# Last block's side work ordered behind four engines' queues, an earlier norm, another bank for the pooled map, and a tail reduction on TensorE

## The chip, the cores and the metric

The kernel runs on one core of a Trainium2 chip. TensorE (PE) multiplies, VectorE (DVE), ScalarE (ACT) and GpSimd (POOL) do the elementwise work, SyncE (SP) issues nearly all transfers. The metric is the device time of one execution in microseconds, as the median of several runs.

## What is computed

One decoder layer on 2048 tokens of width 1024, in float32:

```python
h = rmsnorm(x, norm1)
q, k, v, b_gate, c_gate, hc, p = split(h @ w_in)
attn = sliding_window_attention(q, k, v, sinks, rel_bias)   # window 128, 8 query heads, 2 kv heads
conv = b_gate * causal_conv3(c_gate * hc)
pool = (trailing_mean(p, windows 2/4/8/16) - p) @ pool_w * pool_scale
x = x + concat(attn, conv, pool) @ w_out
x = x + square(relu(rmsnorm(x, norm2) @ w1)) @ w2
out = rmsnorm(x, final_norm)
```

## The kernel before, in words

Every float32 matrix product is made of three TensorE products: an operand is split in a rounded part "hi" and a rest "lo", and `mm3` adds hi·hi, hi·lo and lo·hi in PSUM. ACT makes hi, POOL or DVE the rest. Everything is stored transposed: 128 channels on the partitions, tokens along the free axis.

The first stage goes over four blocks of 512 tokens (`b` = 0 to 3). In a block, `proj` makes 14 tiles in the order of IN_ORDER (k, q0, q1, then, counted by `n` = 0 to 10: v, q2, q3, p0, p1, C0, hc0, B0, C1, hc1, B1), of 24 products each. Attention goes along in eight units: after tile `n`, `att_scores` makes scores on PE and the softmax on DVE and ACT (L581, L588, exp on ACT at L590, L593, L594); two tiles later `att_trans` transposes the unit's probabilities into a `ps_tr` bank and splits them (L604, L607, L608), `att_av` multiplies by v (L615), and `att_out` writes the rows of `mxh` and `mxl` (L623 to L629). `do_pmix` multiplies the pooled values by `pool_w` into a `ps_tr` bank and writes two more rows of `mxh`, `mxl` (L707, L708). Then `out_proj` makes eight tiles, `c` = 0 to 7, each from all eight rows of `mxh` and `mxl`, adds x (L724) and stores to the DRAM tensors `x1s`. PSUM has three banks `ps_mm` for tiles of `proj` and `out_proj`, two `ps_tr`, one `ps_av`, and the score banks.

Between the `out_proj` tiles of block `b` stands the norm of block `b`+1: squares summed by DVE (L374), `norm_rstd` (PE sums over partitions into `pst`, L314; twelve small DVE operations), `row_store` and `norm_bcast` (through DRAM), and `norm_apply` for each of eight channel groups (DVE L404, ACT L405, DVE L406).

Block 3 has no next block. It carries other work for the MLP that follows: `first_rows` and `first_blocks(k, step)`, for `k` = 0 to 3. Step 0 loads four tiles `xb` from `x1s` of blocks 0 and 1, step 1 scales them (four DVE operations, L809), step 2 makes four differences (DVE, L763 with `xb`); the results are stored to `x2s`. FIRST gives for each `k` the tile `n` after which each step is traced. Within `out_proj` of block 3, `first_take` loads them again and splits them (L763 with `hhT`, `hhB`). LAST_DVE puts eight weight splits (L253) of block 3 on DVE instead of POOL.

The order on each engine is not that of the program. The framework schedules at build time with a timing model of its own: when an engine is free in the model, it takes the earliest traced instruction that is ready there, and the queues then run in that fixed order. `tc.issue_after(ins)` adds an edge from each instruction traced within it to `ins`, for instructions on the engine of `ins` alone. Before the change `ins` is the last product of `proj`, a PE instruction, while `first_rows` and `first_blocks` trace only on SP and DVE.

Then comes the MLP in a form with seven products (OPS); `norm2_take` loads its last two operands (T4, B22) once the first stage's memory is free (L965 to L967), and `norm2_rstd` sums block 3's squares (`acc` L732 of POOL). Last comes the second product; its last quarter (256 tokens) is followed by the final norm: four additions to `y` on DVE, four squares on ACT (L1136) and four additions on POOL into `acc3`, `final_rstd`, `final_bcast`, eight `final_mul` on DVE (L1152), each with its store on SP (L1156).

## Time and profile before

| | |
|---|---|
| median of 3 runs | 1938.14 us (1935.13 to 1943.75) |
| profiled execution | 1936.93 us, span 1935.2 us |
| busy: PE, DVE, ACT, POOL | 98%, 58%, 46%, 53% of the span |
| chain that ended last, by engine | PE 83%, DVE 7%, DMA 6%, issue 2% |
| blocks 1, 2 and 3, first product to first product of what follows | 175.88 to 327.52, 479.08 and 648.33 us |

A busy PE includes the pipelined ends of its products, so its share is not its efficiency. An idle time of an engine stands in brackets in a timeline row, with what ended it. The column PEclk of a stretch is the granted TensorE clock: 1.00 is 2.4 GHz, 0.50 is 1.2 GHz.

### The profile page before, as it was taken

Reading aid. Unit: us, or ns where it says so; the run is one execution under the profiler, and the core shown is the slowest. Engines: PE = TensorE matmul, PEld = TensorE weight load, DVE = VectorE, ACT = ScalarE, POOL = GpSimd, SP = SyncE. Lnnn points to the kernel's source line nnn. Section 1 sums busy time; section 2 is a strip of 40 time slices with the busy share of each in tenths; the row PEclk is TensorE's granted clock in tenths of the full one; section 3 lists DMA queues with packets and bytes.
Section 4 is the critical chain, followed back from the end, with each engine's and each line's share of the span. In section 5 each row is a group of like instructions: output and inputs, shape, how many; then the busy total and the mean of one; then the engine's idle time right before and its main releaser. Section 6 shows DMA issues by size and latency. Waiting matters only on the chain.

```text
span 1935.2 us, 25620 instructions
## 1 busy us (share of the span) xinstructions
PE 1892.6 (98%) x8507; PEld 1527.8 (79%) x8507; DVE 1123.6 (58%) x1423; ACT 895.9 (46%) x1640; POOL 1020.0 (53%) x748
## 2 busy tenths in 40 slices
PE   8999999999899999999999999999999999999997
PEld 5877887887687788888888888888888888888887
DVE  5785686585888577756574444442425264533465
ACT  5664674564367344554575545442323222225332
POOL 5666557565463655654464444434565665526521
PEclk9999999999899999999999999999999999999998
DMA  7327316425935779756685655578777566645344
GB/s 255 102 65 225 108 61 217 126 66 174 300 117 178 233 272 335 255 197 212 216 288 194 196 185 189 186 270 279 235 231 240 191 218 200 221 123 169 96 158 134
DMA packets 194136, 373.34 MB, mean 193 GB/s; under 512 B 22167, under 2 KB 30420, under 8 KB 194004
## 3 DMA queue, kind: packets, MB, share of 16 engines
q1 hardware_dynamic: 193768, 371.62, 59.6%
q8 instruction: 67, 1.10, 0.2%
q14 instruction: 65, 0.53, 0.1%
q10 hardware_dynamic: 236, 0.09, 0.0%
HBM read 248.41 MB, written 116.93 MB: 189 GB/s over the span
## 4 chain that ended last, share of the span: by engine, by line
PE 83%; DVE 7%; DMA 6%; issue 2%; ACT 1%; POOL 1%; SPq 1%; DVEq 0%; POOLq 0%; ACTq 0%
PE o L274 11%; PE o L275 11%; PE o L276 11%; PE bT L275 6%; PE bT L276 6%; PE bT L274 6%; PE bB L275 5%; PE bB L274 5%; PE bB L276 5%; PE pj L275 4%; PE pj L276 4%; PE pj L274 4%; DMA x1s<-xo 1%; PE pt L604 1%; DVE xl L406 1%
## 5 line engine op out<-in xcount | busy, mean ns | idle before, releaser
L253 POOL TENSOR_TENSOR wl<-wr,wh 128x512 fp32r<-128x512 f32 x354 | 499.2, 1417 | 502.4 <-ACT wh L252 462.1
L252 ACT CAST wh<-wr 128x512 fp32r<-128x512 f32 x416 | 254.3, 617 | 362.5 <-PE bT L275 66.9
L763 DVE TENSOR_TENSOR bl<-br,bh 128x1024 fp32r<-128x1024 f32 (+2 forms) x144 | 186.8, 1300 | 324.7 <-ACT bh L1111 323.8
L275 PE MATMUL o<-bl,wh 128*128 128x512 f32 (+1 forms) x960 | 363.4, 381 | 0.0
L276 PE MATMUL o<-bh,wl 128*128 128x512 f32 (+1 forms) x960 | 362.7, 381 | 0.0
L274 PE MATMUL o<-bh,wh 128*128 128x512 f32 (+1 forms) x960 | 351.1, 381 | 0.0
L275 PEld LDWEIGHTS o<-bl,wh 128*128 128x128 f32 x960 | 180.9, 188 | 38.3 <-DVE bl L763 0.2
L276 PEld LDWEIGHTS o<-bh,wl 128*128 128x128 f32 x960 | 180.8, 188 | 38.2
L274 PEld LDWEIGHTS o<-bh,wh 128*128 128x128 f32 x960 | 176.3, 188 | 38.0
L276 PE MATMUL bT<-hhT,wl 128*128 128x512 f32 x512 | 203.7, 398 | 0.0
L275 PE MATMUL bT<-hlT,wh 128*128 128x512 f32 x512 | 203.6, 398 | 0.0
L274 PE MATMUL bT<-hhT,wh 128*128 128x512 f32 x512 | 203.4, 398 | 0.0
L274 PE MATMUL pj<-xh,wh 128*128 128x512 f32 x440 | 176.7, 403 | 10.6 <-ACT wh L252 6.7
L275 PE MATMUL pj<-xl,wh 128*128 128x512 f32 x440 | 177.5, 403 | 6.1 <-DVE xl L406 5.8
L276 PE MATMUL pj<-xh,wl 128*128 128x512 f32 x440 | 176.2, 401 | 0.0
L253 POOL TENSOR_TENSOR wl<-s,wh 128x512 fp32r<-128x512 f32 x64 | 91.2, 1426 | 141.5 <-ACT wh L252 130.9
L252 ACT CAST wh<-s 128x512 fp32r<-128x512 f32 x64 | 39.7, 621 | 250.1 <-PE o L275 249.9
L275 PE MATMUL bB<-hlB,wh 128*128 128x512 f32 x384 | 152.3, 397 | 0.7 <-DVE hlB L967 0.7
L274 PE MATMUL bB<-hhB,wh 128*128 128x512 f32 x384 | 152.5, 397 | 0.0
L1111 ACT CAST bh<-br 128x1024 fp32r<-128x1024 f32 (+2 forms) x144 | 123.2, 857 | 63.3 <-PE o L276 57.6
L276 PE MATMUL bB<-hhB,wl 128*128 128x512 f32 x384 | 152.0, 396 | 0.0
L220 POOL TENSOR_TENSOR s<-wr,wr 128x512 f32<-128x512 f32 x64 | 128.5, 2008 | 14.9 <-DMA wr<-in_w_dram 10.2
(188 smaller groups left out, 3388.0 us busy)
## 6 DMA issues: line engine op xcount, KB each, us to landing
wr<-in_w_dram SPq DMA_DIRECT2D x256, 256.0 KB, 3.8
hop_T<-s SPq DMA_DIRECT2D x128, 256.0 KB, 3.1
wr<-in_win_dram SPq DMA_DIRECT2D x112, 256.0 KB, 4.4
hop_B<-h SPq DMA_DIRECT2D x96, 256.0 KB, 3.3
br<-hop_B SPq DMA_DIRECT2D x48, 512.0 KB, 4.4
br<-hop_T SPq DMA_DIRECT2D x48, 512.0 KB, 4.3
wr<-in_wout_dram SPq DMA_DIRECT2D x64, 256.0 KB, 2.9
wr<-ss_T SPq DMA_DIRECT2D x48, 256.0 KB, 2.8
```

Of the source, the lines that this page charges most:

```text
L220: gp.tensor_tensor(out=t, in0=a, in1=b, op=op)
L252: act.copy(hi, src)
L253: eng.tensor_tensor(out=lo, in0=src, in1=f32(hi), op=ALU.subtract)
L274: pe.matmul(ps, hi, xh, start=first, stop=False)
L275: pe.matmul(ps, hi, xl, start=False, stop=False)
L276: return pe.matmul(ps, lo, xh, start=False, stop=last)
L406: dve.tensor_tensor(out=xl[:, k], in0=hf, in1=f32(xh[:, k]), op=ALU.subtract)
L604: pe.transpose(ps[:, m * P : (m + 1) * P], s[:, m, kh * P : (kh + 1) * P], ident)
L763: return dve.tensor_tensor(out=out, in0=a, in1=b, op=ALU.subtract)
L1111: mark["act"] = act.copy(hi, src)
```

## The change

- `behind()` replaces `issue_after(latest)`: an edge to the last instruction traced so far on each of ACT, DVE, POOL and SP. FIRST moves some steps one tile later.
- `norm_rstd`, `row_store`, `norm_bcast` of the next block are traced one `out_proj` tile sooner, and `norm_apply` two groups per tile from `c` = 4 on.
- `do_pmix` takes a `ps_mm` bank.
- At the start of the MLP, `norm2_rstd` and `norm2_row` come one group of seven products later, `norm2_bcast` two products later.
- In the tail ACT's four squares stay apart; `rstd_of` adds them and `acc3` by five accumulating PE products for each 128 tokens, in place of POOL's additions. The eight last stores alternate between SP's and ACT's queues.

```diff
-FIRST = ((0, 1, 2), (0, 3, 4), (3, 5, 6), (5, 7, 8))
+FIRST = ((0, 2, 3), (0, 3, 4), (4, 6, 7), (5, 7, 8))
...
+    sides = {e.engine for e in (act, dve, gp, sp)}
...
+    @contextmanager
+    def behind():
+
+        with ExitStack() as order:
+            seen = set()
+            for ins in reversed(nc.cur_bb.bb.instructions):
+                if ins.engine in sides and ins.engine not in seen:
+                    seen.add(ins.engine)
+                    order.enter_context(tc.issue_after(ins))
+                    if len(seen) == len(sides):
+                        break
+            yield
...
-    def rstd_of(acc, r, offs, psp, tag, name):
+    def rstd_of(accs, r, offs, psp, tag, name):
...
+        accs = accs if isinstance(accs, list) else [accs]
         for j, o in enumerate(offs):
-            pe.matmul(ps[:, j : j + 1], acc[:, o : o + P], ones, start=True, stop=True)
+            for i, acc in enumerate(accs):
+                pe.matmul(ps[:, j : j + 1], acc[:, o : o + P], ones, start=i == 0, stop=i == len(accs) - 1)
...
     def do_pmix(b, i):
         oh, ol = ct["p", i]
-        ps = ps_tr.tile([P, T], F32, tag="tr", name=f"ppm{b}_{i}")
+        ps = ps_mm.tile([P, T], F32, tag="mm", name=f"ppm{b}_{i}")
...
-                with tc.issue_after(latest[0].ins):
+                with behind():
...
-                    for k in range(2 + c * 6 // 2, 2 + (c + 1) * 6 // 2):
+                    for k in range(2 + 3 * c, 5 + 3 * c):
                         norm_square(b + 1, k, dve)
+                    if c:
+                        norm_rstd(b + 1)
                 elif c == 2:
-                    norm_rstd(b + 1)
+                    row_store(nr[b + 1], "n1", (b + 1) * T, T, ps_tr, "tr", f"n1_{b + 1}", tmp(f"row1_{b}"))
                 elif c == 3:
-                    row_store(nr[b + 1], "n1", (b + 1) * T, T, ps_tr, "tr", f"n1_{b + 1}", tmp(f"row1_{b}"))
-                elif c == 4:
                     norm_bcast(b + 1)
                 else:
-                    for k in {5: (0, 1), 6: (2, 3, 4), 7: (5, 6, 7)}[c]:
+                    for k in (2 * (c - 4), 2 * (c - 4) + 1):
                         norm_apply(b + 1, k)
...
-    on((0, 0, 2), norm2_rstd, NB - 1, psb, "b")
-    on((0, 1, 4), lambda: norm2_row(NB - 1, psb, "b", um("row2")))
-    on((0, 3, 0), norm2_bcast, 1)
+    on((0, 1, 2), norm2_rstd, NB - 1, psb, "b")
+    on((0, 2, 4), lambda: norm2_row(NB - 1, psb, "b", um("row2")))
+    on((0, 3, 2), norm2_bcast, 1)
...
-        late.append(lambda: sp.dma_start(outT[f * P : (f + 1) * P, a + cs.start : a + cs.stop], t))
+        late.append(lambda: eng.dma_start(outT[f * P : (f + 1) * P, a + cs.start : a + cs.stop], t))
...
+    acc3[1, 0] = [acc3[1, 0]]
     for j in range(HC):
-        final_square(1, 0, 2 * j + 1, cs, False)
+        if j % 2 == 0:
+            sq = pG.tile([P, TH], F32, tag="sq", name=f"sql_{j}", bufs=2)
+        t = sq[:, j % 2 * w : j % 2 * w + w]
+        act.activation(t, y_of(1, 2 * j + 1, 0, cs), AF.Square)
+        acc3[1, 0].append(t)
     final_rstd(1, 0, cs)
     final_bcast(1, 0, cs)
     for f in range(KC):
-        final_mul(1, 0, f, cs)
+        final_mul(1, 0, f, cs, act if f % 2 else sp)
         flush()
```

## Rows read from the trace of the kernel before

**Rows 1.** The page, busy time by engine: us, share of the span, instructions.

```profile
PE 1892.6 (98%) x8507; PEld 1527.8 (79%) x8507; DVE 1123.6 (58%) x1423; ACT 895.9 (46%) x1640; POOL 1020.0 (53%) x748
```

**Rows 2.** Waits of PE over the whole span: who waited for whom: us in total, times, longest us.

```profile
PE pj L275 <- DVE xl L406: 5.8, 7, 2.9
...
PE pst_n L314 <- POOL acc L942: 3.5, 1, 3.5
...
PE pt L604 <- DVE mxl L708: 2.5, 2, 1.9
...
PE pst_n L314 <- POOL acc L732: 1.2, 1, 1.2
...
PE pj L274 <- DVE bo L653: 0.8, 1, 0.8
```

**Rows 3.** Busy time by stretches: two of block 2 (its start to 378.9; to the end of its last `mxl` row) and three of block 3 (the last begins with the end of its last `mxl` row). Columns: stretch, its length, then PE, PEld, DVE, ACT, POOL busy (instructions), granted clock, DMA share, GB/s.

```profile
327.50:378.90 51.40, 50.52 (x245) 40.72 (x244) 29.13 (x45) 28.56 (x65) 28.62 (x23) 1.00 0.60 167
378.90:440.20 61.30, 60.99 (x304) 50.06 (x303) 49.38 (x64) 42.63 (x98) 39.84 (x41) 1.00 0.19 61
...
479.10:530.50 51.40, 43.38 (x177) 32.98 (x176) 45.62 (x60) 18.62 (x34) 26.80 (x18) 0.90 0.93 297
530.50:608.70 78.20, 74.77 (x364) 60.73 (x364) 66.30 (x86) 52.84 (x127) 41.04 (x35) 0.96 0.34 110
608.70:648.30 39.60, 39.58 (x169) 31.57 (x168) 28.58 (x35) 21.20 (x38) 22.59 (x15) 1.00 0.82 273
```

**Rows 4.** Timeline of DVE in the last `out_proj` tiles of block 2: start us, us, instruction, [idle before <- what ended it].

```profile
474.90 0.75 DVE L809 SCALAR_TENSOR_TENSOR xb<-xb,prm,rb_acc 128x512 f32<-128x512 f32 x1 [5.71 <-DMA xb<-x1s]
475.57 0.68 DVE L724 TENSOR_TENSOR xo<-po,xo 128x512 f32<-128x512 f32 x1
```

**Rows 5.** Stretches with a lower granted clock (columns as in rows 3).

```profile
486.40:493.20 6.80, 3.89 (x9) 2.65 (x9) 6.80 (x7) 1.96 (x4) 3.85 (x3) 0.50 0.86 262
...
595.60:602.40 6.80, 6.35 (x19) 4.95 (x20) 5.87 (x10) 4.40 (x8) 1.28 (x1) 0.50 0.04 15
...
660.50:663.90 3.40, 3.40 (x9) 2.62 (x9) 1.21 (x2) 1.79 (x4) 0.00 (x0) 0.50 0.94 305
...
1923.40:1935.00 11.60, 2.21 (x8) 1.86 (x8) 5.04 (x20) 0.00 (x0) 0.26 (x1) 0.50 0.28 90
```

**Rows 6.** The DVE work of `first_blocks` and what stands beside it. First the durations of half of step 1 and of step 2 (ns, min/median/max, first and last start), then busy time by stretch of one line alone, as DVE (instructions): L809; L763, of which one instruction (0.69 us) is of `first_take`; L253 (DVE, then POOL); and in block 2, from its start to its last `mxl` row, L374 (DVE, then POOL).

```profile
L809 DVE SCALAR_TENSOR_TENSOR xb<-xb,prm,rb_acc x8: 737/752/1776, 474.9 to 529.5; 128x512 f32<-128x512 f32 x8
L763 DVE TENSOR_TENSOR xb<-xb,xb x16: 670/679/1769, 499.1 to 540.6; 128x512 f32<-128x512 f32 x16
479.10:608.70 129.60, 15.65 (x15) 0.93 0.57 184
479.10:608.70 129.60, 13.75 (x17) 0.93 0.57 184
479.10:608.70 129.60, 2.94 (x3) 42.53 (x29) 0.93 0.57 184
327.50:440.20 112.70, 2.31 (x3) 1.30 (x1) 1.00 0.38 109
```

**Rows 7.** DVE's wait for the exponentials, by groups, first in block 2 from 378.9 to 440.2, then in block 3 from 479 to 608 (busy us, mean ns, idle before in us), and three instructions of DVE's timeline: the last softmax step of the third unit of block 2, and the last `mxl` row of block 2 and of block 3.

```profile
L593 DVE RECIPROCAL rd<-den 128x4 f32<-128x4 f32 x5 | 0.9, 178 | 8.9 <-ACT s L590 8.9
...
L593 DVE RECIPROCAL rd<-den 128x4 f32<-128x4 f32 x8 | 1.4, 175 | 8.8 <-ACT s L590 8.8
...
377.18 1.73 DVE L594 TENSOR_TENSOR s<-s,rd 128x1024 f32<-128x1024 f32 x1
439.47 0.69 DVE L629 TENSOR_TENSOR mxl<-ao,mxh 64x512 fp32r<-64x512 f32 x1
608.04 0.69 DVE L629 TENSOR_TENSOR mxl<-ao,mxh 64x512 fp32r<-64x512 f32 x1
```

**Rows 8.** Around the norm between blocks: a row of PE's waits from 176 to 340 us, which holds the first tiles of blocks 1 and 2 (us in total, times, longest); then two rows of the timeline of block 2, DVE's last four sums of squares and PE's reduction of them.

```profile
PE pj L275 <- DVE xl L406: 2.1, 4, 0.6
...
440.19 3.98 DVE L374 TENSOR_TENSOR acc<-acc,sq 128x512 f32<-128x512 f32 x4
...
446.71 0.95 PE L314 MATMUL pst_n<-ones,acc 128*128 128x1 f32 x8
```

**Rows 9.** Timeline of PE and of DVE late in block 0.

```profile
120.13 0.66 PE L604 MATMUL pt<-ident,s 128*128 128x128 f32 x4 [1.85 <-DVE mxl L708]
...
117.21 2.20 DVE L594 TENSOR_TENSOR s<-s,rd 128x1024 f32<-128x1024 f32 x1
```

**Rows 10.** Timeline at the start of the MLP: SP's loads of T4, POOL's share of T4, and PE in B22 (the seventh product).

```profile
656.56 1.89 SPq L965 DMA_DIRECT2D xu_T<-x2s_T  x4
...
665.47 1.50 POOL L967 TENSOR_TENSOR hlT<-xu_T,hhT 128x512 fp32r<-128x512 f32 x1 [0.21 <-ACT hhT L966]
...
670.97 0.50 PE L275 MATMUL bB<-hlB,wh 128*128 128x512 f32 x1 [0.73 <-DVE hlB L967]
```

**Rows 11.** Timeline of the tail: DVE's last additions, PE's reduction, DVE's products, SP's stores.

```profile
1919.52 1.42 DVE L942 TENSOR_TENSOR y<-o,y 128x256 f32<-128x256 f32 x4 [2.70 <-PE o L276]
...
1923.71 1.02 PE L314 MATMUL pst_n<-ones,acc 128*128 128x1 f32 x4 [3.52 <-POOL acc L942]
...
1928.27 3.22 DVE L1152 SCALAR_TENSOR_TENSOR y<-y,prm,pbc_n 128x256 f32<-128x256 f32 x8 [1.38 <-PE pbc_n L356]
...
1928.78 3.77 SPq L1156 DMA_DIRECT2D out_dram<-y  x8
```

More of the change, by code (lines that the diff above doesn't have):

```diff
@@ L1 @@
 import math
-from contextlib import ExitStack
+from contextlib import ExitStack, contextmanager
 import numpy as np
@@ L275, in mm3 @@
         pe.matmul(ps, hi, xl, start=False, stop=False)
-        return pe.matmul(ps, lo, xh, start=False, stop=last)
+        pe.matmul(ps, lo, xh, start=False, stop=last)
     prm = cst.tile([P, NPAR], F32, name="prm")
@@ L482, in tile_trunk @@
     first = {}
-    latest = [None]
     def start_first(tiles):
@@ L510, in proj @@
                     mid()
-                latest[0] = mm3(ps, hi[:, k % HC], lo[:, k % HC], xh[:, k], xl[:, k], k == 0, k == KC - 1)
+                mm3(ps, hi[:, k % HC], lo[:, k % HC], xh[:, k], xl[:, k], k == 0, k == KC - 1)
         return ps
@@ L1142, in final_rstd @@
         r = cst.tile([P, 6], F32, tag="nr3", name=f"r3_{p}_{n}_{cs.start}", bufs=2)[:, : len(offs)]
-        rstd_of(acc3[p, n][:, cs], r, offs, psb, "b", f"n3_{p}_{n}_{cs.start}")
+        a = acc3[p, n]
+        rstd_of([a[0][:, cs]] + a[1:] if isinstance(a, list) else a[:, cs], r, offs, psb, "b", f"n3_{p}_{n}_{cs.start}")
         r3[p, n, cs.start] = r
@@ L1148, in final_bcast, with final_mul @@
         rb3[p, n, cs.start] = bcast(r3[p, n, cs.start], w, psb, "b", f"n3_{p}_{n}_{cs.start}")
-    def final_mul(p, n, f, cs):
+    def final_mul(p, n, f, cs, eng=sp):
         t = y_of(p, f, n, cs)
@@ L1228, in tile_trunk @@
     cs = slice(TH // 2, TH)
+    w = TH // 2
+    acc3[1, 0] = [acc3[1, 0]]
     for j in range(HC):
-        final_square(1, 0, 2 * j + 1, cs, False)
+        if j % 2 == 0:
[3 more added lines that the diff above has]
+        acc3[1, 0].append(t)
     final_rstd(1, 0, cs)
```

## The prediction

> **What bounds the kernel now.** I read the page first: PE is busy for 98% of the span [rows 1], so no edit can win more than the stretches in which PE waits or runs at the lower clock. Next the waits of PE over the span [rows 2]: the reader is to see that they name few places, the norm between blocks (`pj` on `xl`), two banks (`pt` on `mxl`, `pj` on `bo`), and two reductions (`pst` on `acc`). The change touches each of them. Then the busy time by stretch [rows 3]. Block 2 takes 151.6 us (327.5 to 479.1), block 3 takes 169.2 (479.1 to 648.3) for nearly the same products: 17.6 us more, the one large sum in this kernel. In block 3's first 51.4 us PE is busy for 43.4, DVE for 45.6; in the next 78.2 DVE for 66.3. From the last `mxl` row on PE never waits again: 39.6 us for 169 products.
>
> Why block 3 begins badly stands in DVE's timeline [rows 4]: at 474.9, within block 2, DVE runs the first scaling of `first_blocks`, traced in block 3, having sat 5.71 us in front of it for its load. The old edge could not hold it: it bound PE instructions, and that code traces none. The norm's `xl` rows are queued behind. Twice in block 3 PE then runs at 1.2 GHz, 0.50 in the table [rows 5].
>
> All sums below go against the profiled execution, 1936.93 us, which is the span of 1935.2 and 1.7 around it. The median of the runs shown, 1938.14, lies 1.2 above it.
>
> **Norm a tile sooner, blocks 0 to 1 and 1 to 2.** It moves twelve small DVE operations, four PE reductions, a transpose, one store and one load on SP ahead of one tile of 24 products, some 5.6 us. PE waits for `xl` in the first tiles of blocks 1 and 2, 2.1 us in four waits [rows 8]; the rest of the 5.8 in rows 2 is block 3's, below, and block 0's. I take −2.0: `norm_apply` is traced a tile sooner, while the reduction itself ran 2.5 us after its last sum (440.19 + 3.98 against 446.71) and may not move. Ends: −2.1, and +2.4 if PE now reaches both reductions before their sums, at the price of such a wait in rows 2, 1.2 each.
>
> **Pooled map's bank.** Three `mm` banks now serve two more tiles per block. Late in block 0 a transpose waits 1.85 us for the `tr` bank of `do_pmix` [rows 9]; but at that time DVE works without a break (117.21 + 2.20), and what PE does next needs DVE as well. I take 0. Ends: −5.3 (the wait, and half of a 6.8 us stretch at 0.50 as in rows 5), and +1.6, two waits for a projection bank as `pj` on `bo` [rows 2].
>
> **Block 3, the deciding term.** With the new edges step 1 of `k` = 0 may not stand before the last DVE instruction traced at `n` = 2, which is the third unit's L594. In block 2, where PE was hardly held up, that one ends at 377.18 + 1.73 = 378.9, 51.4 us into the block [rows 7]. So the 32 operations of `first_blocks`, which before ran from 474.9 to 541 in time that PE lost [rows 6], move into the attention units, and there DVE has little room: from 378.9 to 440.2 it is busy 49.4 of 61.3 us [rows 3]. All of them are traced before the last unit's `att_out`, so by trace order they come before the last `mxl` row, and no `out_proj` tile can end without that row. The sum for DVE after the first 51.4 us:
> - block 2's work there, 49.4, less its norm sums, 2.3 [rows 3, 6]: 47.1
> - step 1, 15.65 and the one at 474.9 of 0.75; step 2, 13.75 − 0.69 [rows 4, 6]: 29.5
> - weight splits that block 3 has on DVE [rows 6]: 2.9
> - less the overlap of records, about 0.08 each (474.90 + 0.75 against 475.57, rows 4) on 35: −2.8.
>
> That is 76.7 us. Waits for the exponentials cost block 2 8.9 us over five units, 1.8 each [rows 7]; where other work is queued they are filled. Units 5 and 6 have least beside them: 2 × 1.8 = 3.6. The last `mxl` row would be written 51.4 + 76.7 + 3.6 = 131.7 us into the block; before it was 608.7 − 479.1 = 129.6. What remains for PE was 38.9 in block 2 (440.2 to 479.1) and 39.6 in block 3; I take 38.9. Block 3: 170.6 against 169.2, +1.4. The stall at its start goes, and is late again at its end, where PE has run out of projections.
>
> Ends: each of the 32 at its shortest, 16 × 0.737 + 16 × 0.670 = 22.5 (−7.0) [rows 6]; no wait for exponentials (−3.6); 36 of the 192 products done early in three banks, 156 × 0.234 = 36.5 (−2.4): −11.6 in all. Upwards, all 8.9 of waiting (+5.3), 39.6 behind it (+0.7), and 6.8 us at 0.50 behind the wait, as in rows 5 (+3.4): +10.8. Queues: SP's loads of `xb` go behind the stores and loads of tile `n`, so nothing on SP waits for a buffer of the norm any more; POOL and ACT get no instruction from this code, so two of the four edges hold nothing.
>
> The Trainium skill (SBUF — State Buffer, "Who interferes with whom") says that a DVE instruction with two SBUF inputs and a GpSimd one that reads SBUF exclude each other for a whole instruction. The trace agrees: 0.67 to 1.77 us for one form [rows 6]. It speaks against this move: POOL is busy 39.8 of 61.3 us where the work goes and 26.8 of 51.4 where it was [rows 3], 0.65 against 0.52; by the rule the excess of 7.0 us grows by a quarter, and block 3 comes to +3.2 in place of +1.4.
>
> **Start of the MLP.** `norm2_rstd` one group later removes PE's wait of 1.2 for `acc` [rows 2] and, if the clock follows, half of 3.4 us at 0.50 [rows 5]. But T4 and B22 then come 2.9 us sooner, and their loads are issued from 656.56 on, after the memory of the first stage is free; POOL's part of T4 ends at 666.97, and B22 already waits 0.73 [rows 10]. The load is late next. I take −0.6. Ends: −3.7 (1.24 + 1.7 + 0.73) and +1.7, one more stretch at 0.50.
>
> **Tail.** The last addition ends at 1919.52 + 1.42 = 1920.94, its square about 0.45 later at 1921.4, and PE began at 1923.71 [rows 11]. Of ten products of one column (two sets of five) six follow the last square: at 0.95 for four [rows 8] that is 1.4 us, so 1922.9 against 1924.73; at 0.50, 1.02 for two [rows 11], 3.1 and 1924.5. I take −1.6. The stores are issued every 0.47 us (3.77 for eight), the products come every 0.40 (3.22 for eight): two queues give back 0.5. Together −2.1; ends −2.4 and −0.2. The earlier tails with `acc3` are untouched.
>
> **Sum.** −2.0 + 0 + 1.4 − 0.6 − 2.1 = −3.3: 1933.6 for such an execution, 1934.8 for the median.
>
> **Rivals.**
> - The stall is really gone: DVE finds room, block 3 is as long as block 2, −17.6. Sum −22.3, 1916. For it: PE was hardly held up in block 2 with 34 us of DVE idle up to 440.2 [rows 3]. Against it: 22 of these lie before the 51.4 us, where the edges bar the work. Chance 0.20.
> - Slower: DVE falls behind from `n` = 3 on, the waits for exponentials stay unfilled, the last `mxl` row comes at 137, and PE, having waited long, starts the 39.6 us behind it at 0.50 as it ran late in block 3 before [rows 5]. Block 3 +10.8, the rest −4.7: +6.1, 1944. It decides where the new L809 and L763 stand ahead of the next unit's L581 in the queue. For it: the order by trace number. Against it: DVE has filled such waits while it had this work, until 541. Chance 0.16.
> - The edges hold nothing: the instructions behind which they stand are themselves issued early, and the scalings stay in block 2. Then block 3 is unchanged, the rest −4.7, 1933. Chance 0.04.
>
> **How the numbers follow.** The forecast, 0.60, lies at 1935, by itself between 1925 and 1944. About 0.5%, 9.7 us, is what a measurement of this kernel can tell from no change. Faster than that, below 1928.4: the first rival, 0.20, and the favourable part of the forecast (short operations, full banks), 0.13: 0.33. Slower, above 1947.8: half of the second rival, with the clock against it, 0.08. The same: 0.59. The range reaches to the first rival and past the second: 1917 to 1946.
>
> **What would show it.** No L809 before the third unit's L594, and waits of PE on `xl` at block 3's start gone: the edges work. The last `mxl` row of block 3 some 130 us after its first product, with `av`, `pt` or `po` waiting for DVE before it: the forecast; at 115 or less, the first rival. The `pst` wait near 657 gone and T4 or B22 waiting longer on `hlT`, `hlB`; `pst` of the tail within 2 us after the last addition. Block 3 shorter than 158 or longer than 180 us would make the prediction's main step wrong.

## The result, and the profile after

The changed kernel takes 1948.59 us (median of 6 runs, 1947.14 to 1951.16) beside 1939.62 for the kernel before in the same comparison: ratio 1.0049, 95% interval 1.0034 to 1.0064. It is slower by some 9 us; the forecast was 1934.8, its range ended at 1946. The profiled execution took 1951.16, its span is 1949.4. It is the slowest of the six, and the one profiled before, 1936.93, lies 2.7 below its median: the two traces lie 14.2 us apart, the medians 9.0.

The page's busy times, beside [rows 1]:

```profile
PE 1900.1 (97%) x8523; PEld 1535.8 (79%) x8523; DVE 1125.0 (58%) x1423; ACT 897.9 (46%) x1640; POOL 1015.2 (52%) x744
```

The work is the same to 8 us. What is new stands in PE's waits over the whole span, beside [rows 2] (us in total, times, longest):

```profile
PE ppm L288 <- ACT poh L711: 13.3, 5, 5.2
PE sc L590 <- DVE s L594: 6.9, 2, 4.4
...
PE po L288 <- DVE xo L737: 3.1, 1, 3.1
...
PE pj L289 <- DVE xl L422: 1.5, 2, 1.1
...
PE bT L289 <- POOL hlT L980: 1.0, 1, 1.0
...
PE pst_n L330 <- ACT sql L1249: 0.3, 1, 0.3
```

Of the waits that the change was aimed at, `pj` on `xl` fell from 5.8 to 1.5, `pt` on `mxl` (2.5) is no longer in the list, and the two waits of `pst` on `acc` are gone. In their place PE waits for `poh`, the high part of the pooled map, 13.3 us in five places, 8.9 of it in block 3, and 6.9 us for the softmax (`s`); neither wait stands in the list before. Busy time by stretch, beside [rows 3] (blocks 1 and 2; block 3 in three parts, cut 51.4 us after its start and at the end of its last `mxl` row):

```profile
179.90:335.60 155.70, 152.63 (x718) 123.33 (x716) 103.60 (x142) 87.90 (x193) 95.26 (x83) 0.99 0.44 128
335.60:489.20 153.60, 151.03 (x717) 122.22 (x716) 103.77 (x142) 86.97 (x190) 94.90 (x83) 1.00 0.42 124
489.20:540.60 51.40, 50.74 (x247) 41.36 (x246) 27.60 (x45) 28.26 (x65) 28.27 (x24) 1.00 0.70 196
540.60:623.90 83.30, 68.73 (x302) 54.95 (x301) 75.31 (x95) 41.27 (x94) 37.18 (x28) 0.90 0.50 168
623.90:666.40 42.50, 39.43 (x163) 31.31 (x162) 29.61 (x37) 23.36 (x42) 23.71 (x17) 0.96 0.85 287
```

The reader is to see two things. At the start of block 3 the stall is gone: PE is busy for 50.74 of its first 51.4 us, where it was 43.38. And everything behind is longer: 83.3 us to the last `mxl` row (78.2 before), with PE busy for 68.73 and the clock at 0.90, then 42.5 (39.6 before). Blocks 0, 1, 2 and 3 take 179.9, 155.7, 153.6 and 177.2 us, against 175.9, 151.6, 151.6 and 169.2; the MLP up to its second product 632.3 (635.0), the rest 650.7 (651.9). That adds up to the 14.2 us between the traces, not to the 9 between the medians.

The edges do what they say. DVE's timeline has the first scaling right behind the third unit's softmax, and the last `mxl` row 134.7 us into block 3:

```profile
538.32 1.73 DVE L607 TENSOR_TENSOR s<-s,rd 128x1024 f32<-128x1024 f32 x1
539.97 0.74 DVE L822 SCALAR_TENSOR_TENSOR xb<-xb,prm,rb_rb 128x512 f32<-128x512 f32 x1
...
622.83 1.15 DVE L642 TENSOR_TENSOR mxl<-ao,mxh 64x512 fp32r<-64x512 f32 x1 [0.68 <-ACT mxh L641]
```

### The profile page after: what moved, and what is told of

Same layout as the page of the kernel before. It is cut to its first block, busy times and chain, and to the rows that moved or that the text cites. A ratio compares the mean times of both kernels' runs of the same rounds, so it can differ in the third digit from the quotient of the medians.

```text
span 1949.4 us, 25646 instructions
## 1 busy us (share of the span) xinstructions
PE 1900.1 (97%) x8523; PEld 1535.8 (79%) x8523; DVE 1125.0 (58%) x1423; ACT 897.9 (46%) x1640; POOL 1015.2 (52%) x744
## 4 chain that ended last, share of the span: by engine, by line
PE 73%; DVE 5%; DMA 3%; issue 1%; ACT 1%; SPq 0%; POOL 0%; DVEq 0%; ACTq 0%; POOLq 0%
PE o L288 11%; PE o L289 11%; PE o L290 11%; PE bT L290 6%; PE bT L289 6%; PE bT L288 6%; PE bB L288 4%; PE bB L289 4%; PE bB L290 4%; PE pj L289 2%; PE pj L290 2%; PE pj L288 2%; PE po L289 1%; PE po L288 1%; PE po L290 1%
## 5 line engine op out<-in xcount | busy, mean ns | idle before, releaser
L253 ACT CAST wh<-wr 128x512 fp32r<-128x512 f32 x416 | 254.4, 618 | 415.1 <-POOL wl L254 69.8
L288 PEld LDWEIGHTS o<-bh,wh 128*128 128x128 f32 x960 | 176.3, 188 | 38.6 <-ACT bh L1124 0.4
L290 PE MATMUL pj<-xh,wl 128*128 128x512 f32 x440 | 178.3, 406 | 0.0
L253 ACT CAST wh<-s 128x512 fp32r<-128x512 f32 x64 | 39.7, 621 | 250.2 <-PE o L289 250.2
L288 PE MATMUL bB<-hhB,wh 128*128 128x512 f32 x384 | 152.5, 397 | 0.0
L289 PE MATMUL bB<-hlB,wh 128*128 128x512 f32 x384 | 152.1, 396 | 0.0
L290 PE MATMUL bB<-hhB,wl 128*128 128x512 f32 x384 | 152.0, 396 | 0.0
```

The source lines that it names most:

```text
L253: act.copy(hi, src)
L288: pe.matmul(ps, hi, xh, start=first, stop=False)
L289: pe.matmul(ps, hi, xl, start=False, stop=False)
L290: pe.matmul(ps, lo, xh, start=False, stop=last)
```

## The experiments

All times are medians in us, each ratio against the kernel before on the same chip with its 95% interval. The stage lengths are those of one profiled execution each, so they add up only to a few us. How far one execution is to be trusted can be read where the code of a block is the same: in the thirteen kernels whose TensorE queue has the same order over the first 150 us (before, e1, e4, e6 to e8, e10 to e12, e15 to e18) block 0 takes 174.5 to 176.3 us, and 178.1 in e6; block 2 takes 151.6 in the kernel before and 153.2 in e8, which changes nothing up to there. "n" counts the projections of a block as above, and "dw tiles" are those that it counts.

| kernel | time | ratio | blocks 0, 1, 2, 3 | last `mxl` in block 3 |
|---|---|---|---|---|
| before | 1937.6 to 1939.7 | 1 | 175.9, 151.6, 151.6, 169.2 | 129.6 |
| after | 1948.59 | 1.0049 [1.0034, 1.0064] | 179.9, 155.7, 153.6, 177.2 | 134.7 |
| e1: after, old bank | 1941.61 | 1.0012 [1.0002, 1.0023] | 174.5, 154.4, 150.6, 173.3 | 130.3 |
| e2: after, old edge | 1951.93 | 1.0065 [1.0047, 1.0082] | 178.5, 156.3, 155.7, 174.2 | 132.9 |
| e3: before, new bank | 1946.46 | 1.0039 [1.0024, 1.0054] | 179.4, 155.6, 152.9, 168.8 | 127.6 |
| e4: before, new edges | 1946.18 | 1.0031 [1.0018, 1.0044] | 176.3, 152.0, 153.0, 175.7 | 132.4 |
| e5: after, products ordered later | 1962.17 | 1.0125 [1.0111, 1.0140] | 184.2, 157.2, 158.2, 174.9 | 130.9 |
| e6: e1, side work early | 1950.58 | 1.0067 [1.0050, 1.0085] | 178.1, 153.9, 150.6, 178.9 | 138.9 |
| e7: before, norm sooner | 1941.09 | 1.0016 [1.0005, 1.0027] | 175.3, 154.7, 150.0, 168.7 | 129.1 |
| e8: before, MLP start and tail | 1938.44 | 1.0002 [0.9992, 1.0012] | 175.0, 151.4, 153.2, 169.6 | 130.2 |
| e9: after, products traced last | 1952.32 | 1.0067 [1.0055, 1.0080] | 176.2, 155.9, 156.8, 176.3 | 132.9 |
| e10: before, side work early, splits ordered | 1942.92 | 1.0020 [1.0011, 1.0029] | 175.8, 151.9, 152.4, 169.1 | 129.2 |
| e11: before, side work early | 1940.96 | 1.0011 [1.0000, 1.0021] | 175.0, 153.0, 153.5, 168.1 | 128.1 |
| e12: before, splits ordered | 1942.14 | 1.0019 [1.0010, 1.0029] | 174.8, 151.9, 153.4, 169.0 | 129.6 |
| e13: after, second product alone in `mm` | 1955.37 | 1.0080 [1.0065, 1.0095] | 175.9, 156.4, 154.7, 180.1 | 131.1 |
| e14: after, first product alone in `mm` | 1950.05 | 1.0053 [1.0038, 1.0069] | 176.9, 155.0, 153.6, 178.3 | 131.0 |
| e15: before, differences on GpSimd | 1937.58 | 0.9993 [0.9982, 1.0003] | 175.0, 152.5, 153.0, 167.6 | 129.1 |
| e16: before, no differences | 1935.61 | 0.9975 [0.9964, 0.9985] | 176.1, 151.9, 152.4, 165.5 | 125.8 |
| e17: combined | 1937.91 | 0.9994 [0.9985, 1.0003] | 175.0, 151.6, 152.9, 169.0 | 129.4 |
| e18: combined, tighter | 1942.27 | 1.0019 [1.0008, 1.0029] | 174.9, 152.1, 154.6, 168.6 | 128.3 |

**e1 and e2: one part undone in the changed kernel.** e1 takes the product's bank back, e2 the edges and their schedule.

```
# e1, in do_pmix
-        ps = ps_mm.tile([P, T], F32, tag="mm", name=f"ppm{b}_{i}")
+        ps = ps_tr.tile([P, T], F32, tag="tr", name=f"ppm{b}_{i}")
# e2
-                with behind():
+                with tc.issue_after(latest[0].ins):
-FIRST = ((0, 2, 3), (0, 3, 4), (4, 6, 7), (5, 7, 8))
+FIRST = ((0, 1, 2), (0, 3, 4), (3, 5, 6), (5, 7, 8))
```

> The kernel after with the pooled map's product back in a ps_tr bank, all else as changed. Theory 1 (the bank move is what costs: the first of the three ppm products, which needs only poh, is queued on PE as soon as poh is ready in the framework's model, and PE then stands behind it, 13.3 us in five waits of PE on poh, with a lower clock behind the long ones): these waits fall below 2 us in total, blocks 0 to 2 are each 2 to 4 us shorter than in the kernel after, and the time falls by 8 to 14 us, to 1935 to 1941. Theory 2 (DVE's room in block 3 is what costs, the bank is incidental): block 3 stays at 174 to 178 us and the time falls by less than 5 us.

> The kernel after with the old edge (to a PE instruction, which holds nothing here) and the old FIRST, all else as changed. Theory 1: the waits on poh stay in blocks 0 to 2, block 3 falls by no more than 3 us, the time stays above 1944. Theory 2: the side work fills DVE's early idle time again, block 3 goes from 177 back to about 169 us and the time falls by 6 to 9 us, to 1940 to 1943.

e1 gives back 7 of the 9 us, a little less than theory 1 wanted: the bank is the larger loss. In e1 no wait of `ppm` on `poh` is left; in e2 they stay (10.4 us in five), and PE also waits 5.3 us for an `xl` part at block 3's start, since the scaling stands in block 2 again (its first start, 481.95, lies 8.6 us ahead of block 3). So with the new bank in place, taking the edges back gains nothing, as theory 1 said: 1.0065 beside 1.0049, with intervals that overlap. The difference can be read in PE's timeline. In e1, late in block 0, projections stand between the steps of attention without a pause:

```profile
97.82 0.28 PE L591 MATMUL sc<-Kd,q 128*128 128x256 f32 x1
97.94 0.39 PE L290 MATMUL pj<-xh,wl 128*128 128x512 f32 x1
98.18 0.40 PE L288 MATMUL pj<-xh,wh 128*128 128x512 f32 x1
...
102.84 0.39 PE L290 MATMUL pj<-xh,wl 128*128 128x512 f32 x1
103.08 0.60 PE L617 MATMUL pt<-ident,s 128*128 128x128 f32 x4
```

In the changed kernel the same stretch holds no projection at all:

```profile
95.92 0.39 PE L629 MATMUL av<-ptl,VV 128*128 128x512 f32 x1
98.87 0.58 PE L590 MATMUL sc<-Kd,q 128*128 128x256 f32 x1 [2.56 <-DVE s L594]
...
102.88 0.79 PE L628 MATMUL av<-pth,VV 128*128 128x512 f32 x1 [1.94 <-DVE ao L637]
...
104.43 1.97 PE L617 MATMUL pt<-ident,s 128*128 128x128 f32 x8 [0.32 <-DVE s L607]
106.28 0.79 PE L288 MATMUL ppm<-poh,pwh 128*128 128x512 f32 x1
106.87 0.63 PE L288 MATMUL pj<-xh,wh 128*128 128x512 f32 x1
```

The projection comes right behind the first matmul of `ppm`, which waits for the pooled map. Without projections PE follows attention's chain through DVE and ACT step by step, and the granted clock falls to 0.50 for 10.2 us from 98.7 on; in the 3.4 us before, PE was busy for 1.01:

```profile
95.30:98.70 3.40, 1.01 (x8) 0.69 (x6) 3.40 (x3) 2.79 (x10) 1.23 (x1) 0.99 0.23 77
98.70:108.90 10.20, 7.77 (x24) 5.99 (x25) 9.98 (x16) 4.49 (x13) 6.21 (x5) 0.50 0.00 1
```

**e3 and e4: one part alone on the kernel before**, by the same edits the other way round.

> The kernel before with the pooled map's product in a ps_mm bank and nothing else. Theory 1: waits of PE on poh appear in all four blocks (6 us or more in total), and the time is 5 to 10 us above the kernel before, 1944 to 1950. Theory 2: within 3 us of the kernel before.

> The kernel before with the new edges and the new FIRST and nothing else. Theory 1: block 3 changes by less than 3 us and the time by less than 3. Theory 2 (the sum of the prediction): the stall at the start of block 3 goes, its last mxl row comes 130 us or more into the block, block 3 takes 170 to 178 us against 169, and the time is 1 to 8 us above the kernel before.

Each alone costs 6 to 8 us, as theory 1 said of e3 and theory 2 of e4. In these executions the bank costs blocks 0 to 2 3.5, 4.0 and 1.3 us and leaves block 3 alone; the edges cost block 3 6.4 us and leave the others within 1.4. Beside the new edges the bank costs block 3 as well: 177.2 in the changed kernel, 173.3 in e1.

**e5: the bank kept, the products placed later by an order on PE.**

```
-                do_pmix(b, 0)
-            elif n == 9:
-                do_pmix(b, 1)
+            elif n in (8, 10):
+                with behind(pe):
+                    do_pmix(b, n // 2 - 4)
```

> The changed kernel with its pooled-map products still in the projection banks; only their place in the program moves: the first unit's is traced with the first pair's dw tile n = 8, the second's with n = 10, and both are ordered behind TensorE's latest instruction, so that the builder cannot lift them to a place where the pooled map does not stand yet. Theory A (the loss comes from where the builder puts the products in TensorE's queue, ahead of poh; the bank itself costs nothing): the waits of ppm on poh, 13.3 us in the changed kernel, fall below 2 us, blocks 0 to 2 come back to about 175, 152 and 151 us, and the time is about 1941 us, as with the products in the old bank (1941.6). Theory B (one projection bank fewer holds the projections up by itself): the waits on poh go, but waits of the projections' first products on the evictions of their banks take their place, block 0 stays near 179 us, and the time stays at 1946 to 1949 us.

Both theories missed: it is worse by 14 us than the changed kernel. The waits for `poh` went, as theory A wanted, and others took their place, which theory B did not name:

```profile
PE av L628 <- DVE ao L637: 18.7, 7, 7.0
```

PE still has no projection beside attention. The order of its queue says why. In block 0 of the kernel before the last three projections (n = 8, 9 and 10) start at 94.19, 102.09 and 110.00, the first product at 110.93. In the changed kernel the first product starts at 106.28, and the projection of n = 8, traced next in that pool, right behind its first matmul at 106.87. Here the product's matmuls start at 122.40 to 123.25, and the next projection, n = 9, at 123.68. This led to theory C: a pool gives out its banks in the order of the program, so whatever comes next in the pool can't start before the product has. The traces bear that order out in all four blocks of all seven kernels with a product in `mm` (the changed kernel, e2, e3, e5, e9, e13, e14); in the kernel before and e1 the first tile of `out_proj` starts ahead of the second product in every block.

**e6: e1 with the side work early**, counted from block 3's first projection, still behind all four engines.

```
+    def side_work(m):          # m counts IN_ORDER; called behind each projection of block 3
+        with behind():
+            if m == 0:
+                first_rows()
+            ...
-FIRST = ((0, 2, 3), (0, 3, 4), (4, 6, 7), (5, 7, 8))
+FIRST = ((0, 2, 3), (0, 3, 4), (4, 5, 6), (5, 6, 7))
```

> The changed kernel with the products back in the old bank (1941.6 us, block 3 173.3 us) and the last block's side work traced earlier: it is counted from the block's first projection, its rows and loads behind that one, its twelve block steps at the third to tenth of the projection and dw tiles, each still ordered behind the latest instruction of the four side engines. Theory 2 (block 3 is long because the blocks fall into the part where VectorE has no room): the last row of mxl comes at 117 to 124 us of the block instead of 130 to 135, block 3 takes 156 to 163 us and the time is 1926 to 1933 us, below both kernels. Rival (the block's start has no room either: the blocks push the projections' hi and lo parts, or the evictions, late): waits of the projections on xl and of dw on q and ql take 5 us and more, the last row of mxl comes no earlier than 128 us, and the time is 1938 us or more.

The rival held in its times, by the wait on q and not by one on `xl`. Eight loads now stand on SP's queue ahead of the hops of K and q; SP's timeline, then PE's:

```profile
493.59 6.12 SPq L816 DMA_DIRECT2D xb<-x1s  x8
500.12 0.33 SPq L198 DMA_DIRECT2D wr<-in_win_dram  x1
500.78 1.33 SPq L546 DMA_DIRECT2D Kd<-Kd  x2
```

```profile
512.61 0.55 PE L590 MATMUL sc<-Kd,q 128*128 128x256 f32 x1 [6.51 <-DMA q<-ql]
```

The hop of K leaves 18.2 us into the block (500.78 − 482.6); in e1 it left at 489.47, 10.0 us in. The last `mxl` row comes later, not sooner. So an edge to four engines also orders SP, and PE loses 6.5 us by it. A second wait of 6.5 us, of a projection for `ct` of ACT at 578.35 (2.3 in e1), is not accounted for.

**e7 and e8: the remaining parts alone on the kernel before.** e7 is the norm's new tile indices, e8 the later norm2 steps and the new tail.

> The kernel before with the norm one tile sooner and nothing else. The forecast's own term: the 3.0 us wait at 595.6 us falls by about 2 us, blocks 0 to 2 change by less than 2 us each, and the time is 1936 to 1939 us beside 1939.6. Rival (with the old edge the block steps are lifted to the end of block 2, and a norm that comes sooner there gives them room to go ahead of the last xl parts): the wait of block 3's first projections on xl is 4 us and more, and the time is 1941 us or more.

> The kernel before with the later norm2 steps at the start of the MLP and the new tail (squares summed by TensorE, stores from two queues), and nothing else. Forecast: the tail gives 1 to 2.5 us, the start of the MLP 0.6 us at most, so 1936.5 to 1938.6 us beside 1939.6. Rival (the tail's products wait for the squares and the squares for their buffer, so nothing is gained): 1939.6 us, and the tail's last sum comes as late behind the last addition as before.

e7 makes the kernel slower by 3 us. PE's timeline of e7 shows the reduction of the norm and then the first waits of block 1, which starts at 175.30:

```profile
143.38 0.95 PE L314 MATMUL pst_n<-ones,acc 128*128 128x1 f32 x8
...
182.04 0.50 PE L275 MATMUL pj<-xl,wh 128*128 128x512 f32 x1 [2.13 <-DVE xl L406]
183.73 0.50 PE L275 MATMUL pj<-xl,wh 128*128 128x512 f32 x1 [0.73 <-DVE xl L406]
```

The reduction starts 31.9 us ahead of the block, as before (143.96 and 175.88): tracing it sooner did not move it. What did move is the order of the `xl` parts: the last one ends 8.4 us into block 1, before at 6.8, and the clock drops for 3.4 us. Block 1 takes 3.1 us more; block 2 gains 1.6, where the last comes at 5.1 instead of 6.3. But the four blocks of this execution end at 648.61, before at 648.33, and the 2 us by which its trace is longer lie in the MLP, which e7 does not change. So what its 3 us are made of is not shown. e8 is no difference in time, as its rival said: the last stage is shorter by 2.3 us, the MLP's first longer by 1.1.

**e9: the products traced behind the last two dw tiles**, with no order of their own.

```
-                do_pmix(b, 0)
-            elif n == 9:
-                do_pmix(b, 1)
+            if n in (9, 10):
+                do_pmix(b, n - 9)
```

> The changed kernel with its pooled-map products still in the projection banks, but traced with the last two dw tiles, n = 9 and n = 10, and with no order of its own. Theory C (the banks of one pool are taken in the order of the program, so a projection that is traced behind a product cannot start before that product's first matmul has been placed; TensorE then has no projection to put between the steps of attention): only the last projection is now behind a product, the others stand beside attention again, blocks 0, 1 and 2 come back to 174 to 177, 153 to 155 and 150 to 152 us, the waits of ppm on poh and of av on ao are 3 us in total at most, and the time is 1940 to 1943 us, as with the products in the old bank (1941.6). Theory B (a bank more in use costs by itself, wherever the products stand): the blocks stay at 179, 155 and 153 us and the time at 1946 to 1949 us.

A miss for theory C's numbers, though not for its mechanism: in block 0 the last projection starts at 109.67, right behind the product's first matmul at 109.45, and the two others are back at 93.60 and 101.52. Block 0 is back at 176.2 us, blocks 1 and 2 are not. I had taken one projection behind a product to be harmless. The waits speak against that: it is the last one that PE has to put between the last units of attention (`av` on `ptl`, 5.2 us in one wait in block 3). The second product now stands ahead of `out_proj` besides (126.61 and 127.20).

**e13 and e14: one product in `mm`, the other in `tr`.** e13 has the second there, traced behind the last projection; e14 the first, in its place of the change.

```
-        ps = ps_mm.tile([P, T], F32, tag="mm", name=f"ppm{b}_{i}")
+        ps = ps_mm.tile(...) if i == 1 else ps_tr.tile(...)     # e13; i == 0 in e14
-            elif n == 9:
+            elif n == 10:                                       # e13 alone
```

> The changed kernel with only the second unit's pooled-map product in a projection bank, traced with the last dw tile (n = 10) so that no projection is behind it in that pool; the first unit's product is in the old bank. Theory C (order of the pool: a projection traced behind a product can't start before it): no projection is held, blocks 0, 1 and 2 take 174 to 176, 153 to 155 and 150 to 152 us, and the time is 1940 to 1943 us. Theory B (each product in a projection bank costs by itself): half of the 7 us, about 1945 us, with blocks 1 us each above those.

> The changed kernel with only the first unit's pooled-map product in a projection bank, in its place of the change (behind n = 7, so that three projections are behind it); the second unit's product is in the old bank. Theory C: TensorE waits for poh in every block as in the changed kernel (1.2 to 5 us each), blocks 0 and 1 come to 178 to 180 and 155 to 157 us, and the time is 1945 to 1949 us, most of the 7 us. Theory B: half of it, about 1945 us, and about the same as with the second product alone.

In time theory C missed with both: 1955.37 where it had 1940 to 1943, 1950.05 where it had 1945 to 1949, and in e14 PE waits for `poh` in block 3 alone. In the queue it holds in both. In e14 the product starts at 107.25 in block 0 and the next projection at 107.84; in e13 the projections stand in the order of e1, and the product at 127.04 is followed by the first tile of `out_proj` at 127.61, which in e1 starts at 117.15, ahead of the second product. `out_proj` draws from the same pool, and I had left it out. The cost is the same whichever tile is held: from 80 to 120 us of blocks 1 and 2, PE loses (sum over its matmuls of the time to the next start, less the median for that kind and shape in the first stage, 0.23 us for 512 columns) some 0.6 us in the kernel before, e1, e4 and e7, and 2.4 to 2.6 in the changed kernel, e3, e13 and e14. So the two products don't add up, and theory B's "half each" is wrong too. That any one product in `mm` costs this much, whatever it holds, is not excluded: no run has a product there with nothing behind it in the pool. Much of e13's high time is made at the end of block 3, by one wait of the MLP's first product for a bank whose last sum is late (e14 has it too, 5.4):

```profile
PE bB L288 <- DVE xo L737: 6.5, 1, 6.5
```

**e10, e11, e12: a free start for the loads, DVE's order alone.** On the kernel before, the scalings and differences go behind DVE's latest instruction from the second tile on, rows and loads are free (e11); the splits of `first_take` go behind the latest of DVE and ACT (e12); e10 has both.

```
+    def side_work(m):
+        if m == 0:
+            first_rows()
+        for k, at in enumerate(FIRST):     # ((0, 1, 2), (0, 3, 4), (4, 6, 7), (5, 8, 9))
+            for step in range(3):
+                if m == at[step]:
+                    with behind(*([dve] if step else [])):
+                        first_blocks(k, step)
...
-                    first_take(i)
+                    with behind(dve, act):
+                        first_take(i)
```

> The kernel before with the last block's side work placed by two new orders and nothing else: rows and loads are free, the scaling and sums of the blocks go behind VectorE's latest instruction alone, from the second tile of the block on (steps 1 and 2 at tiles 1 and 2, 3 and 4, 6 and 7, 8 and 9), and each split of a loaded tile (NEARLY's part in the output projection) goes behind the latest instruction of VectorE and ScalarE. Theory 2 (VectorE's room decides): the first xl waits of block 3 (5.3 us before) fall below 2 us, no xb comes before the block's own xl parts, the part from 100 to 120 us loses 2 us instead of 5.6 since the splits no longer stand in it, block 3 takes 155 to 163 us, and the time is 1925 to 1933 us. Rival (the loads and stores of the blocks on SP's queue hold the hops of K and q, as where the loads went first): a wait of sc on q or Kd of 4 us or more near 25 to 40 us of the block, block 3 at 168 us or more, and the time at 1938 us or more.

> As the kernel with both new orders, but the splits of the loaded tiles keep their old freedom. If the start of the block is what matters (theory 2, first half), block 3 is within 3 us of the kernel with both; if the splits are (they take VectorE and ScalarE between 60 and 120 us), block 3 is 4 us or more longer than with both, and the loss at 100 to 120 us stays at 5 us or more.

> The kernel before with only the splits of the loaded tiles ordered behind the latest instruction of VectorE and ScalarE. If the splits are what block 3 loses at 100 to 120 us, its 5.6 us there fall to 2 and the time is 1934 to 1936 us; the waits at the block's start stay. Rival: the splits move to where VectorE adds the output projection, the MLP waits for the last of them, and the time is 1938 us or more.

None is faster. Their four blocks end within 1.3 us of the kernel before (649.0 to 649.6 beside 648.3); most of what their traces lose lies in the MLP up to its second product, 637.6 to 638.2 us beside 635.0, where PE waits 3.2 to 4.1 us for the sum of squares `acc` instead of 1.2. Where the loads are free they start at 470.60 in e11, ahead of block 3, and K's hop leaves 13.7 us into it, not 18.2 as in e6. The busy times of e11 show what happens (block 3's first 60 us, and from there to its last `mxl` row):

```profile
481.50:541.50 60.00, 56.79 (x272) 45.93 (x271) 48.70 (x64) 30.37 (x68) 32.17 (x25) 1.00 0.79 238
541.50:609.60 68.10, 57.73 (x267) 45.21 (x267) 62.69 (x79) 39.77 (x91) 32.76 (x26) 0.95 0.39 132
```

The start is good, PE busy for 56.79 of 60 us (51.98 in the kernel before), and the second part gives it back, 57.73 of 68.1 (66.17 of 69.6). The splits are innocent: ordering them left PE's loss from 100 to 120 us of block 3, counted as for e13, where it was (5.6 in e12 beside 5.7 in the kernel before, 8.7 in e10 beside 8.6 in e11) and cost some 2 to 4 us.

**e15, e16: less of DVE's work.** On the kernel before, the sixteen differences go to GpSimd (e15) or are left out (e16).

```
         def sums():
+            # e15: sub = gp.tensor_tensor for p == 0; e16: no sub for p == 0
             sub(b11, b12, b11)
```

> The kernel before with the sixteen differences of the last block's blocks (xb<-xb,xb: 13.4 us of VectorE within block 3) on GpSimd instead of VectorE, and nothing else. Theory 2 (VectorE's work is what block 3 is long by): VectorE's busy time in the block's first 130 us falls from 112 to about 99 us, block 3 takes 160 to 165 us, the time is 1928 to 1934 us, below before. Rival (GpSimd needs 1.3 to 1.6 us for each, 21 to 26 us beside its own 68, and the lo parts of the weights come late): waits of pj on wl appear, block 3 stays at 168 us or more, the time at 1938 us or more.

> The kernel before without the sixteen differences of the last block (the four sums of each step are stored unsummed, so the first pass of the MLP gets other inputs); all loads, scalings and stores stay. It measures what 13.4 us of VectorE's work are worth in block 3. Theory 2: 5 to 10 us, block 3 at 159 to 164 us and the time at 1928 to 1933 us. Rival (block 3 is bound by the chain of attention and by the loads' queue, not by VectorE's work): under 2 us, 1936 us or more.

Taking 13.4 us of DVE's work out of block 3 shortens it by 3.8 us (165.5) and the kernel by 0.25%, 4 to 5 us: less than theory 2 wanted, more than its rival. On GpSimd they take 1.29 us each instead of 0.68, and the gain is not measurable.

**e17, e18: a version meant to beat both.** The kernel before with e8's parts, e11's order and e15's engine. In e18 the scalings stand at tiles 1, 2, 4 and 6, each unit's differences right behind them; the stores of the plain blocks then come behind the differences that overwrite two of them, so that part of what the MLP gets is changed.

```
-FIRST = ((0, 1, 2), (0, 3, 4), (4, 6, 7), (5, 8, 9))    # e17
+FIRST = ((0, 1, 1), (0, 2, 2), (2, 4, 4), (3, 6, 6))    # e18
```

> A version meant to beat both: the kernel before with the new tail and MLP start (no difference by themselves), the scalings of the last block's blocks behind VectorE's latest instruction from its second tile on (without the start's xl waits, which took 8.5 us), and the sixteen differences on GpSimd (13.4 us of VectorE less). If VectorE's full stretch from 80 to 120 us was what gave the early placement's gain back, the loss there falls from 11 to 12 us to 6 us or less, block 3 takes 158 to 163 us, and the time is 1929 to 1934 us. Rival (the end of the attention stage loses this with VectorE free too): the loss there stays above 9 us, block 3 at 166 us or more, the time at 1937 us or more.

> As the other combined kernel, with the scalings at tiles 1, 2, 4 and 6 of the block and each unit's differences traced right behind them, so that the last scaling is done by about 55 us instead of 90. If an early end of the side work is worth something beyond the amount, block 3 is 2 to 4 us shorter than there, 155 to 160 us, and the time is 1926 to 1932 us. Rival (the early loads and stores on SP's queue hold the hops of K and q): sc waits for q or Kd 3 us or more near 25 to 45 us of the block, and the time is no less than there.

e17's rival held; e18's held in its time, but not by the wait that it named (`sc` on q 1.8 us there, not 3). e17 beats the changed kernel by some 11 us and equals the kernel before. Its block 3, in the same two parts:

```profile
479.50:539.50 60.00, 56.16 (x262) 44.85 (x261) 39.29 (x54) 29.34 (x67) 39.69 (x32) 0.97 0.82 247
539.50:608.90 69.40, 61.60 (x281) 48.38 (x280) 61.06 (x73) 40.43 (x94) 47.59 (x35) 0.93 0.38 126
```

DVE is idle for 20.7 of the first 60 us, and yet in the second part PE misses 7.8 of 69.4. So neither the place nor the amount of DVE's side work accounts for all that block 3 is longer by. What holds the second part in e17 stays open; PE's waits there name `pt` on `mxl` (2.6 us), `sc` on `s` (2.5), `pj` on `bo` (1.5) and `av` on `ao` (0.8), all ended by DVE, and no run took those away.

## Why the prediction was wrong

**Pooled map's bank: the step that failed.** "I take 0. Ends: −5.3 [...] and +1.6" was wrong by more than its own bounds: the bank costs 7 us (e1 against the changed kernel; 7 to 8 alone, e3). I had asked who waits for the bank that is left and how often the bank that is taken would be missing. I had not asked what else is taken from that pool behind the product in the program. What the traces show in place of a wait for a free bank is the place in PE's queue: the tile that is next in the pool starts only behind the product, and the product waits for `poh` (13.3 us) in the stretch in which PE needs projections to cover attention.

**Block 3: mechanism right, one term wrong.** The edges hold, the `xl` waits at the start are gone, and the sum for DVE came out: 76.7 us of work were forecast behind the first 51.4, 75.31 are in the second part of block 3 above. The last `mxl` row was forecast at 131.7 us and came at 132.4 in e4, 130.3 in e1 and 134.7 with the bank's losses on top (8.9 us of waits for `poh`). The term that failed is the remainder behind it, taken as 38.9 because in the kernel before "PE never waits again" there. It took 43.3 in e4, 43.1 in e1 and 42.4 here. DVE's timeline of the changed kernel shows what PE waited for: splits of `first_take` stand in front of an addition of `out_proj`, and behind that stands PE. They come later than before (the last starts 157.3 us into the block, before 149.8), as do the stores that they need: the last to `x2s_T` leaves at 618.4, before at 542.1. That the late stores are the reason is read from this order; no run tested it.

```profile
642.37 3.59 DVE L776 TENSOR_TENSOR hlT<-xt,hhT 128x512 fp32r<-128x512 f32 x4
645.88 0.68 DVE L254 TENSOR_TENSOR wl<-wr,wh 128x512 fp32r<-128x512 f32 x1
646.48 0.68 DVE L776 TENSOR_TENSOR hlT<-xt,hhT 128x512 fp32r<-128x512 f32 x1
647.08 0.68 DVE L737 TENSOR_TENSOR xo<-po,xo 128x512 f32<-128x512 f32 x1
```

```profile
647.90 0.52 PE L288 MATMUL po<-mxh,wh 128*128 128x512 f32 x1 [3.07 <-DVE xo L737]
```

So the edges cost block 3 6.4 us alone (e4) where +1.4 was forecast, within the ends of −11.6 and +10.8. The rule of the Trainium skill that I weighed there (SBUF — State Buffer, "Who interferes with whom") would have given +3.2; no run separates its share.

**Norm sooner.** −2.0 was forecast with ends −2.1 and +2.4; alone it is +3 (e7). I wrote that the reduction "may not move", and it did not. Of the `xl` waits of the kernel before, what blocks 1 and 2 leave is all block 3's (3.8 us); block 0 has none. With the edges in place it may help block 3: e1, which has it, takes 173.3 there and is at 1.0012, e4 without it (and without the new tail) 175.7 and 1.0031; no run adds the norm alone to the edges.

**MLP start and tail.** −0.6 and −2.1 were forecast; together they measure +0.4 us, −1.6 to +2.3 (e8), with the stages at +1.1 and −2.3. The tail's share came near its forecast: from the second product to the end the eleven kernels with the new tail take 649.6 to 651.2 us, the nine with the old one 651.4 to 653.0, on average 1.9 more. In the tail the reduction begins before the last addition ends, and the last of its products ends 2.5 us behind it (1938.08 + 1.53 against 1937.07; it was 3.8), with a granted clock of 0.64 over its last 1.6 us. The timeline of the changed kernel:

```profile
1935.65 1.42 DVE L955 TENSOR_TENSOR y<-o,y 128x256 f32<-128x256 f32 x4 [2.70 <-PE o L290]
...
1936.64 1.35 PE L330 MATMUL pst_n<-ones,sql 128*128 128x1 f32 x8 [0.32 <-ACT sql L1249]
...
1938.08 1.53 PE L330 MATMUL pst_n<-ones,sql 128*128 128x1 f32 x8
```

**The rivals.** "The stall is really gone" fell with block 3 at 177.2, "the edges hold nothing" with the first scaling at 539.97. The slower rival, 1944, was nearest: it had the last `mxl` row at 137 and block 3 at +10.8, and 134.7 and +8.0 came, with lower clocks behind waits. But it decided on the order within DVE, and most of the loss came from the bank, which no rival held. The 9.7 us that the prediction takes as the least that can be told from no change were too many: the interval of the whole change leaves out 1.0 at 9 us, that of e16 at 5.

## What to carry to other kernels

Before moving a tile to another pool, list everything that the program takes from that pool behind it: in a build that hands out buffers in program order, as the queues of seven kernels here show it, each of these now waits for the tile's inputs, and a "free bank" says nothing about that. A stage in which several engines take turns is repaired only when its last term is: here a good start of block 3 (4 to 8 us more of PE's work) came back as a worse end in each placement that had it (e1, e4, e11, e17). And test each part of a change alone and left out: the single losses here add up to 17 us, the whole change to 9, and taking back one of two losses gave 7 us (e1) or nothing (e2).

## What the runs showed that was not expected

An edge to the latest instruction of several engines also orders the queue of loads: eight loads of 256 KB ahead of a hop made it 8 us later (e6). A short wait can cost twice: after the 2.56 us wait at 96.31 PE's granted clock was 0.50 for 10.2 us, and the scores behind it followed one another in 0.21 us instead of 0.12. But it need not. The thirteen kernels with the same TensorE queue at the start have the same wait of 1.8 to 1.9 us at about 120 us (`pt` on `mxl`, [rows 9]). In e1, e7, e11, e12, e17 and e18 the clock stayed at 1.00 behind it; at 0.50 it stood for 3.4 us in e8 and e15 (in e10 only from 129.2 us on), for 6.8 in the kernel before, for 10.2 in e4, e6 and e16. First e1, then e6 (the stretch with the wait, and the one behind it):

```profile
117.90:121.30 3.40, 1.59 (x8) 1.07 (x8) 3.37 (x4) 1.23 (x3) 2.49 (x2) 1.00 0.12 35
121.30:131.50 10.20, 7.21 (x31) 5.11 (x32) 8.92 (x17) 6.98 (x12) 2.73 (x3) 1.00 0.16 49
```

```profile
120.00:123.30 3.30, 1.45 (x9) 1.07 (x8) 3.27 (x4) 1.27 (x3) 2.55 (x3) 1.00 0.10 37
123.30:133.50 10.20, 8.35 (x22) 5.69 (x22) 7.58 (x15) 5.41 (x9) 2.66 (x3) 0.50 0.15 44
```

So one trace alone does not give the price of a wait.

And 13.4 us less work on an engine that is busy for 112 of 130 us gave 4 to 5 us; moving that work to an engine with room, at twice the time each, gave nothing that can be measured.
